# A two-layer hybrid trunk on one core: the delta rule's keys, values and output in three passes of 256 columns, and sums of ones read in turn from two stretches

## The chip, the core and the metric

The kernel runs on one core of a Trainium2 chip. The metric is the device time of one execution in microseconds. Five engines work side by side, each running its own list of instructions in order and waiting for the others by semaphores: PE (TensorE, matrix products into PSUM; its weight loads are shown apart as PEld), DVE (VectorE), ACT (ScalarE), POOL (GpSimd) and SP (SyncE, which here issues the loads of the weights).

## What is computed

Two layers on 256 tokens of 2,048 channels, all in float32: differential attention, then a gated MLP with a causal convolution (the FFN); a gated delta rule, then another such FFN. The change lies in the delta rule:

```python
def gated_deltanet(h, w_in, conv_w, a_log, dt_bias, norm_g, w_out):
    proj = h @ w_in
    qkv, z, b_gate, a_gate = jnp.split(proj, [...], axis=-1)
    qkv = jax.nn.silu(causal_dwconv(qkv, conv_w))
    q, k, v = jnp.split(qkv, [GDN_KEY_DIM, 2 * GDN_KEY_DIM], axis=-1)
    q = l2_norm(q.reshape(b_sz, s_len, GDN_QK_HEADS, GDN_HEAD_DIM).astype(jnp.float32))
    k = l2_norm(k.reshape(b_sz, s_len, GDN_QK_HEADS, GDN_HEAD_DIM).astype(jnp.float32))
    ...
    o = gated_delta_rule(q, k, v, g, beta)
    o = rms_norm(o, norm_g) * jax.nn.silu(z.reshape(b_sz, s_len, GDN_V_HEADS, GDN_HEAD_DIM).astype(jnp.float32))
    return o.reshape(b_sz, s_len, GDN_VALUE_DIM).astype(h.dtype) @ w_out
```

The rule itself (`gated_delta_rule`) solves a unit lower triangular system of 64 x 64 for each chunk of 64 tokens and head, and carries a state from chunk to chunk. There are 16 key heads and 32 value heads of 128.

## The kernel before, in words

**Float32 from two halves.** A float32 matrix product is made of products of a rounded type (`fp32r`). A weight chunk `raw` comes from memory, ScalarE rounds it to `whi` (L88), VectorE keeps the rest as `wlo` (L89). Activations are kept the same way: a main half ah and a small half al, side by side as 2 x 256 tokens. The product is hi·ah + lo·ah + hi·al. In `dense` one *step* (one of kt tiles of 128 input channels, one of 2 tiles of 128 output channels) is a pair: hi against ah and al together, 512 columns, into a whole bank of the accumulator `ps` (L114), then lo against ah, 256 columns, onto its first half (L115). So the first half of the bank holds the main sum and the second half hi·al. Every matmul comes with a load of its weights.

**Reading in turn.** `turns` makes the moving operand alternate between token j and token 128 + j, so the columns of `ps` come out interleaved; `halves` undoes that with a view that steps by two.

**After a dense product.** `merge` (L127) brings the halves together: ScalarE copies the small half out (L134), VectorE adds the main half (L135) and multiplies by the row's norm `rstd` (L136). For output products `add_x` (L242) adds the two halves to the residual x with two VectorE instructions (L245). `total` (L234) sums over the 128 channels of a partition axis with a matmul against ones (L239), the summed operand again in two halves. There it is read straight through.

**The delta rule** (`gdn`) goes over 4 blocks of 4 key heads. For each block: four dense products for keys and queries (`w_in`, 16 x 2 steps each), one for the first values, two products for the gate z (`dense_tok`, L151 to L153, three matmuls of 512 columns a step), three more for the values; then the output products of the block before (`w_out`, 8 products of 8 x 2 steps). The last block's own output closes the layer. Beside it run generators that `tick` steps once per weight chunk: `keys` (norms by L239, ScalarE's logarithms and exponentials at L500 to L506, VectorE's L507, products L514 and L515), `to_tokens` (transposes L604, ScalarE copy L605), `invert` (a loop of small VectorE instructions L542 and L545 that inverts 32 x 32 blocks, closed by two transposes L549 and L551), and `group`, which first joins the blocks (`levels`: L570, L579, L581, L589, L595) and then makes the products L625, the norm of the result (L648, L649, logarithm and exponential L226 and L227, behind a table load L207), the gate multiply L659, the transposes L669 and the operand `oc` of the output product (L672, L673). These small products go to tiles `mp`. The gate z itself leaves `ps` by ScalarE's L704.

**Buffers.** `ps` has two buffers, `mp` four, `raw`, `whi` and `wlo` three each. A chunk of weights is four tiles of 128 input channels for `dense` (8 steps) and two for `dense_tok`.

**What sets the order.** The framework's scheduler puts the instructions of each engine into a list by its own estimate of when each could run. A change of a few matmuls therefore moves others. The weights of every engine's list are consumed in the same sequence, so the place of an instruction can be told by the chunks around it.

Of the kernel before, what the change touches and what calls it, by code (L numbers as in the profile page):

```python
# [10 lines left out]
AF = mybir.ActivationFunctionType  # L11
ALU = mybir.AluOpType
# [4 lines left out]
P = 128  # L17
T = 256
D = 2048
KD = D // P  # L20
EPS = 1e-6
CK = 4
HP, AP, OP = 40, 48, 112
# [3 lines left out]
class Trunk:  # L27
# [71 lines left out]

    def dense(self, w, kt, acts, place, tiles=2, lead=0, dist=(45, 45)):  # L100


        nc = self.nc
        ps = self.banks()
        for k0, nk in self.chunks(kt, CK, lead):
            hi, lo = self.weights(w[:, k0:k0 + nk, :], [(place - x) % P for x in dist])
            steps = [(k, c) for k in range(nk) for c in range(tiles)]
            if k0 + nk == kt:
                steps = [(k, c) for c in range(tiles) for k in range(nk)]
            for k, c in steps:  # L110
# [3 lines left out]
                nc.tensor.matmul(ps[:, c, :], hi[:, k, s], self.turns(a), start=first, stop=False)  # L114
                nc.tensor.matmul(ps[:, c, :T], lo[:, k, s], self.turns(a[:, :1, :]), start=False, stop=last)  # L115
            self.tick()
        return ps
# [8 lines left out]

    def merge(self, ps, u):  # L127

        nc = self.nc
        n = u.shape[1]  # L130
        main, small = self.halves(ps[:, :n])
        t = self.sp.tile([P, 2, T], F32, tag="mt", name="mt", bufs=1)[:, :n]
        v = "p c (q j) -> p c q j"
        nc.scalar.copy(t.rearrange(v, q=2), small)  # L134
        nc.vector.tensor_tensor(u.rearrange(v, q=2), main, t.rearrange(v, q=2), ALU.add)  # L135
        nc.vector.tensor_tensor(u, u, self.rstd.unsqueeze(1).to_broadcast([P, n, T]), ALU.mult)  # L136
# [97 lines left out]
    def total(self, out, parts):  # L234

        n = len(parts)
        for i, p in enumerate(parts):
            for j in range(2):
                last = self.nc.tensor.matmul(out, self.onesr, p[:, j], start=i + j == 0, stop=i + j == n)  # L239
        return last  # L240

    def add_x(self, k, n, ps):  # L242
        x = self.x[:, k:k + n, :].rearrange("p c (q j) -> p c q j", q=2)
        for part in self.halves(ps):
            self.nc.vector.tensor_tensor(x, part, x, ALU.add)  # L245

    def add_out(self, blk, ps, done):

        self.add_x(2 * blk, 2, ps)
# [46 lines left out]
    def attention(self, w_qk, w_v, w_o, nh, dist_ap, ident_ap, qg, kg, lvec, sub, start, done, lambda_init):  # L296

        nc, mp = self.nc, self.mp
        with self.tc.tile_pool(name="at", bufs=1) as at:
# [34 lines left out]
            def normed(ps, gain):  # L334
                r = at.tile([P, 2, T], F32, tag="qkr", name="qkr", bufs=3)
                self.merge(ps, r)
                sq = squares(r)
                qn = at.tile([P, 2, T], F32, tag="qkn", name="qkn", bufs=4)

                def go():  # L340
                    yield
                    pn = mp()
                    self.total(pn, [sq])
                    ri = at.tile([P, 2, T], F32, tag="ri", name="ri", bufs=2)
                    self.rsqrt(ri, pn, P)
# [38 lines left out]
            def values(h, v, aT):  # L384
# [11 lines left out]
                ri = at.tile([P, 2, T], F32, tag="ri", name="ori", bufs=2)  # L396
                self.rsqrt(ri[:, 0, :], pn[:, :T], 2 * P)
                for e in range(2):
# [30 lines left out]
    def gdn(self, w_gate, w_in, w_z, w_out, nb, hb, gate_ap, const_ap, hot_ap, conv_col, ng, done):  # L429
# [12 lines left out]
        with tc.tile_pool(name="gd", bufs=1) as gd:  # L442
# [32 lines left out]
            def keys(hq, c, cc, b0, res):  # L475
# [201 lines left out]
            def out(b, acts):  # L677
                for blk in range(KD // 2):
                    ps = self.dense(w_out[b * (KD // 2) + blk], 2 * hb, lambda k: self.await_(acts, k), OP)
                    self.add_out(blk, ps, done if b == nb - 1 else None)  # L680

# [3 lines left out]
            for b in range(nb):  # L685
# [6 lines left out]
                for op, i in plan + [("v", i) for i in range(1, hb)]:  # L692
                    if op == "k":
                        hq = heads[i]
                        c = convs(lin(self.dense(w_in[hq * 2], KD, self.h_acts, HP)), (hq, nq + hq))
                        self.spawn(keys(hq, c, cc, 2 * i, lqs))
# [9 lines left out]
                    else:  # L706
                        gi = i // gh
                        gr = groups[gi]
                        if i == gr[0]:
# [3 lines left out]
                        hq = heads[i]  # L713
                        c = convs(lin(self.dense(w_in[hq * 2 + 1], KD, self.h_acts, HP)),
                                  (2 * nq + 2 * hq, 2 * nq + 2 * hq + 1))
# [208 lines left out]
```

## Time and profile before

| | |
|---|---|
| median of 3 runs | 2615.27 us (2613.68 to 2615.49) |
| profiled execution | 2612.84 us, its span 2611.1 us |
| mean granted TensorE clock | 0.987 |
| HBM | 476 MB read, 183 GB/s over the span |
| attention and its output, 0 to 320 us | PE busy 309.14 of 320 us |
| FFN of layer 0, in part, 420 to 1060 us | PE busy 640.00 of 640 us |
| delta rule, 1060 to 1892 us | PE busy 794.2 of 832 us |
| FFN of layer 1, 1892 to 2612 us | PE busy 714.42 of 720 us |

The times of matmuls in the trace overlap, since they are pipelined: the distance between the starts of two matmuls is what one of them costs. A window row gives its length, then each engine's busy time and number of instructions, the granted clock, the DMA share and GB/s. The delta rule's sum is that of five windows (64.31, 211.21, 199.02, 205.00 and 114.70 us). The rows on which the prediction rests stand with it.

### The profile page before, as it was taken

To read this page: it belongs to the slowest core of one execution; us is meant where nothing else is said; L and a number is where in the kernel's file an instruction comes from. 1 tells how busy PE (TensorE), PEld (TensorE's weight loads), DVE (VectorE), ACT (ScalarE), POOL (GpSimd) and SP (SyncE) were. 2 spreads that over 40 slices of the span, in tenths; PEclk is the share of its full clock that TensorE was granted. 3 is DMA by queue.
4 is the path that set the end of the run, shared out by engine and by line. 5 is a ranking of instruction groups with operands and counts; after the bars stand their busy time and mean duration, and the time that the engine had idled before them with its cause. 6 is when DMAs were issued, how large, how long until landed. Compare 5 with 4: busy or idle time off the path is not lost.

```text
span 2611.1 us, 41169 instructions
## 1 busy us (share of the span) xinstructions
PE 2557.8 (98%) x15904; PEld 2328.6 (89%) x15904; DVE 1945.4 (75%) x2911; ACT 1510.2 (58%) x2119; POOL 107.2 (4%) x221
## 2 busy tenths in 40 slices
PE   8999999999999999999979999999899999999999
PEld 7998899999999999889969989978799999999998
DVE  7776677778887555789679779779587788776554
ACT  6666656666666444685564674574366666665333
POOL 0000000000000000031021020120100000000000
PEclk9999999999999999999989999999799999999999
DMA  6555565666556666556425446445256556656665
GB/s 211 179 182 177 167 205 199 201 201 201 202 200 203 199 203 200 193 171 194 154 97 194 145 155 200 149 159 170 73 182 202 201 201 201 201 201 206 210 208 169
DMA packets 135412, 480.81 MB, mean 184 GB/s; under 512 B 15408, under 2 KB 18480, under 8 KB 135216
## 3 DMA queue, kind: packets, MB, share of 16 engines
q1 hardware_dynamic: 134064, 475.58, 55.9%
q8 instruction: 124, 2.03, 0.3%
q10 hardware_dynamic: 1152, 2.61, 0.3%
q14 instruction: 72, 0.59, 0.1%
HBM read 476.03 MB, written 2.10 MB: 183 GB/s over the span
## 4 chain that ended last, share of the span: by engine, by line
PE 95%; ACT 2%; DVE 1%; DMA 1%; issue 1%; SPq 0%; ACTq 0%; DVEq 0%
PE ps L114 54%; PE ps L115 27%; PE ps L151 3%; PE ps L153 3%; PE ps L152 3%; PE mp L625 2%; PE mp L239 1%; PE mp L515 1%; ACT whi L88 0%; DMA raw<-w_in 0%; PE mp L595 0%; PE mp L589 0%; DVE wlo L89 0%; PE mp L604 0%; DMA raw<-w_qk 0%
## 5 line engine op out<-in xcount | busy, mean ns | idle before, releaser
L89 DVE TENSOR_TENSOR wlo<-raw,whi 128x1024 fp32r<-128x1024 f32 (+2 forms) x909 | 1104.2, 1215 | 535.4 <-ACT whi L88 521.8
L88 ACT CAST whi<-raw 128x1024 fp32r<-128x1024 f32 (+2 forms) x909 | 945.2, 1040 | 892.2 <-PE ps L114 767.2
L114 PE MATMUL ps<-h,whi 128*128 128x512 f32 x4304 | 1427.0, 385 | 19.1 <-ACT zt L704 9.7
L115 PE MATMUL ps<-h,wlo 128*128 128x256 f32 x4304 | 1182.7, 275 | 2.2 <-DVE wlo L89 2.2
L114 PEld LDWEIGHTS ps<-h,whi 128*128 128x128 f32 x4304 | 818.8, 190 | 135.0 <-ACT zt L704 10.8
L115 PEld LDWEIGHTS ps<-h,wlo 128*128 128x128 f32 x4304 | 831.4, 193 | 5.1 <-DVE wlo L89 3.6
L114 PE MATMUL ps<-ac,whi 128*128 128x512 f32 x1632 | 535.1, 382 | 0.0
L115 PE MATMUL ps<-ac,wlo 128*128 128x256 f32 x1632 | 444.8, 273 | 0.0
L114 PEld LDWEIGHTS ps<-ac,whi 128*128 128x128 f32 x1632 | 308.4, 189 | 43.1 <-issue 0.2
L115 PEld LDWEIGHTS ps<-ac,wlo 128*128 128x128 f32 x1632 | 313.3, 192 | 0.1
L114 PE MATMUL ps<-oc,whi 128*128 128x512 f32 x512 | 171.0, 387 | 0.9 <-DVE oc L673 0.9
L152 PE MATMUL ps<-wlo,h 128*128 128x512 f32 x384 | 145.7, 379 | 1.4 <-DVE wlo L89 1.4
L151 PE MATMUL ps<-whi,h 128*128 128x512 f32 x384 | 146.2, 381 | 0.9 <-ACT whi L88 0.9
L153 PE MATMUL ps<-whi,h 128*128 128x512 f32 x384 | 145.9, 380 | 0.0
L220 DVE SCALAR_TENSOR_TENSOR cv<-u,fcols,cv 128x255 f32<-128x255 f32 (+1 forms) x344 | 142.7, 477 | 0.0
L115 PE MATMUL ps<-oc,wlo 128*128 128x256 f32 x512 | 141.1, 276 | 0.0
L114 PEld LDWEIGHTS ps<-oc,whi 128*128 128x128 f32 x512 | 98.2, 192 | 15.1 <-DVE oc L673 1.3
L115 PEld LDWEIGHTS ps<-oc,wlo 128*128 128x128 f32 x512 | 99.5, 194 | 0.1
L218 ACT ACTIVATE cv<-u,fcols 128x256 f32<-128x256 f32 x172 | 93.9, 593 | 0.6 <-DVE u L136 0.5
L245 DVE TENSOR_TENSOR x<-ps,x 128x512 f32<-128x512 f32 (+1 forms) x114 | 77.0, 676 | 16.5 <-PE ps L115 15.4
L220 DVE SCALAR_TENSOR_TENSOR cv<-u,cols,cv 128x255 f32<-128x255 f32 (+2 forms) x192 | 84.5, 477 | 1.9 <-ACT cv L216 1.8
L136 DVE TENSOR_TENSOR u<-u,rstd 128x512 f32<-128x512 f32 x118 | 81.7, 692 | 3.3
(200 smaller groups left out, 1850.7 us busy)
## 6 DMA issues: line engine op xcount, KB each, us to landing
raw<-w_up SPq DMA_DIRECT2D x344, 512.0 KB, 4.7
raw<-w_down SPq DMA_DIRECT2D x160, 512.0 KB, 3.7
raw<-w_in SPq DMA_DIRECT2D x128, 512.0 KB, 4.6
raw<-w_z SPq DMA_DIRECT2D x64, 512.0 KB, 3.5
raw<-w_out SPq DMA_DIRECT2D x64, 512.0 KB, 4.6
raw<-w_qk SPq DMA_DIRECT2D x63, 512.0 KB, 4.6
raw<-w_v SPq DMA_DIRECT2D x32, 512.0 KB, 3.5
raw<-w_o SPq DMA_DIRECT2D x32, 512.0 KB, 4.7
```

The costliest lines, as they stand in the source:

```text
L88: nc.scalar.copy(hi, raw)
L89: nc.vector.tensor_tensor(lo, raw, hi.bitcast(F32), ALU.subtract)
L114: nc.tensor.matmul(ps[:, c, :], hi[:, k, s], self.turns(a), start=first, stop=False)
L115: nc.tensor.matmul(ps[:, c, :T], lo[:, k, s], self.turns(a[:, :1, :]), start=False, stop=last)
L136: nc.vector.tensor_tensor(u, u, self.rstd.unsqueeze(1).to_broadcast([P, n, T]), ALU.mult)
L151: nc.tensor.matmul(ps[:, c, :], ah, wh, start=first, stop=False)
L152: nc.tensor.matmul(ps[:, c, :], ah, wl, start=False, stop=False)
L153: nc.tensor.matmul(ps[:, c, :], al, wh, start=False, stop=last)
L218: nc.scalar.activation(out, u, AF.Identity, bias=bias, scale=taps[n - 1])
L220: nc.vector.scalar_tensor_tensor(out[:, j:], u[:, :T - j], taps[n - 1 - j], out[:, j:], ALU.mult, ALU.add)
L245: self.nc.vector.tensor_tensor(x, part, x, ALU.add)
L625: nc.tensor.matmul(p[:, v, :], l(v), r[:, v, :], start=i == 0, stop=i == len(terms) - 1)
```

## The change

`dense` gets a switch `wide`. With `wide=False` a step is three matmuls of 256 columns onto the same half bank: hi·ah, lo·ah, hi·al, each read in turn from two stretches as before. The products for keys, queries, values and output of the delta rule use it; attention, the two FFNs, the decay gates and the gate z keep what they had. `merge` of such a product is one VectorE multiply from `ps` by `rstd`, `add_x` one addition. `total` reads its operand in turn, through `pairs`; its result is then interleaved, and `apart` gives the view that undoes it.

```diff
-    def dense(self, w, kt, acts, place, tiles=2, lead=0, dist=(45, 45)):
+    def dense(self, w, kt, acts, place, tiles=2, lead=0, dist=(45, 45), wide=True):
...
+        n = 2 * T if wide else T
...
-                nc.tensor.matmul(ps[:, c, :], hi[:, k, s], self.turns(a), start=first, stop=False)
-                nc.tensor.matmul(ps[:, c, :T], lo[:, k, s], self.turns(a[:, :1, :]), start=False, stop=last)
+                nc.tensor.matmul(ps[:, c, :n], hi[:, k, s], self.turns(a[:, :n // T, :]), start=first, stop=False)
+                nc.tensor.matmul(ps[:, c, :T], lo[:, k, s], self.turns(a[:, :1, :]), start=False, stop=last and wide)
+                if not wide:
+                    nc.tensor.matmul(ps[:, c, :T], hi[:, k, s], self.turns(a[:, 1:, :]), start=False, stop=last)
...
-    def merge(self, ps, u):
+    def merge(self, ps, u, wide=True):
...
+        if not wide:
+            r = self.rstd.rearrange("p (q j) -> p q j", q=2).unsqueeze(1).to_broadcast([P, n, 2, P])
+            nc.vector.tensor_tensor(u.rearrange(v, q=2), main, r, ALU.mult)
+            return
...
-                last = self.nc.tensor.matmul(out, self.onesr, p[:, j], start=i + j == 0, stop=i + j == n)
+                last = self.nc.tensor.matmul(out, self.onesr, self.pairs(p[:, j]), start=i + j == 0, stop=i + j == n)
...
+    def pairs(self, a):
+
+        return a.rearrange("p c t -> p t c") if len(a.shape) == 3 else a.rearrange("p (c t) -> p t c", c=2)
+
+    def apart(self, ps):
+
+        return ps.rearrange("p (t c) -> p c t", c=2)
+
-    def add_x(self, k, n, ps):
+    def add_x(self, k, n, ps, wide=True):
         x = self.x[:, k:k + n, :].rearrange("p c (q j) -> p c q j", q=2)
-        for part in self.halves(ps):
+        for part in self.halves(ps)[:1 + wide]:
             self.nc.vector.tensor_tensor(x, part, x, ALU.add)
...
-                self.merge(ps, u)
+                self.merge(ps, u, False)
...
-                    nc.scalar.activation(sq[:, 0, :], pn[:, :T], AF.Ln, bias=eps128, scale=float(P))
-                    nc.scalar.activation(sq[:, 1, :], pn[:, T:], AF.Ln, bias=self.eps, scale=1.0)
+                    pq, pk = self.apart(pn)[:, 0, :], self.apart(pn)[:, 1, :]
+                    nc.scalar.activation(sq[:, 0, :], pq, AF.Ln, bias=eps128, scale=float(P))
+                    nc.scalar.activation(sq[:, 1, :], pk, AF.Ln, bias=self.eps, scale=1.0)
...
-                        c = convs(lin(self.dense(w_in[hq * 2], KD, self.h_acts, HP)), (hq, nq + hq))
+                        c = convs(lin(self.dense(w_in[hq * 2], KD, self.h_acts, HP, wide=False)), (hq, nq + hq))
```

The two logarithms of attention (L345 and L397) take the view of `apart` in the same way, and the products for values and output get `wide=False` like the keys.

In the scheduler's lists the attention and the FFN stand as before, but in the delta rule nearly every small instruction moves. Three places follow; line numbers of the new kernel are higher (L704 is L721 there, L605 is L621, L542 and L545 are L558 and L561, L549 and L551 are L565 and L567, L570 is L586, L595 is L611, L604 is L620; its dense matmuls are L115, L116 and L118, its merge L138).

ScalarE at the end of the key heads of block 2; `zt<-ps` is the gate leaving the accumulator, `vt` the first values. Before:

```order
L505 ACTIVATE d<-d 128x256
L506 ACTIVATE d<-mp,gc 128x128
L502 ACTIVATE qs<-qs 128x512
L605 COPY vt<-mp 128x2x256
L704 ACT_TABLE_LOAD
L704 ACTIVATE zt<-ps,rstd 128x512 x4
L88 CAST whi<-raw 128x1024 x4
```

Now:

```order
L521 ACTIVATE d<-d 128x256
L522 ACTIVATE d<-mp,gc 128x128
L621 COPY vt<-mp 128x2x256
L721 ACT_TABLE_LOAD
L721 ACTIVATE zt<-ps,rstd 128x512 x2
L88 CAST whi<-raw 128x1024 x5
L721 ACTIVATE zt<-ps,rstd 128x512 x2
L88 CAST whi<-raw 128x1024 x5
```

Both z products left the accumulators in one go, with no rounding of weights between; now five chunks are rounded between the first and the second. It is so in blocks 2, 3 and 4; in block 1 the two were already apart.

VectorE at the end of the inversion of block 4; `x<-ps` is an output product added to the residual, `u<-ps,rstd` the new merge. Before:

```order
L245 TENSOR_TENSOR x<-ps,x 128x512
L542 TENSOR_TENSOR tmp<-X,Ti 128x30
L89 TENSOR_TENSOR wlo<-raw,whi 128x1024
L545 TENSOR_TENSOR Ti<-Ti,tmp 128x30
L549 STREAM_TRANSPOSE ttc<-Ti 128x32x32
L551 STREAM_TRANSPOSE tcc<-Ti 128x32x32
L89 TENSOR_TENSOR wlo<-raw,whi 128x1024
L245 TENSOR_TENSOR x<-ps,x 128x512
```

Now:

```order
L558 TENSOR_TENSOR tmp<-X,Ti 128x30
L561 TENSOR_TENSOR Ti<-Ti,tmp 128x30
L565 STREAM_TRANSPOSE ttc<-Ti 128x32x32
L567 STREAM_TRANSPOSE tcc<-Ti 128x32x32
L89 TENSOR_TENSOR wlo<-raw,whi 128x1024
L138 TENSOR_TENSOR u<-ps,rstd 128x512
L89 TENSOR_TENSOR wlo<-raw,whi 128x1024
L227 SCALAR_TENSOR_TENSOR cv<-u,cols,cv 128x255
```

The inversion ended between the last additions of block 3's output; now it ends while the values of block 4 are merged and convolved, 18 weight chunks earlier.

PE in the inversion levels of block 4. Before:

```order
L579 MATMUL mp<-ttc,pc 32x32 x2
L581 MATMUL mp<-pc,TT 32x32
L589 MATMUL mp<-Ta,lt 64x64 x8
L595 MATMUL mp<-TT,lq 64x64 x8
L570 MATMUL mp<-tcc,lt 32x32 x16
L604 MATMUL mp<-con,cv 128x128 x4
L579 MATMUL mp<-ttc,pc 32x32 x2
```

Now:

```order
L118 MATMUL ps<-oc,whi 128x256
L115 MATMUL ps<-oc,whi 128x256
L116 MATMUL ps<-oc,wlo 128x256
L611 MATMUL mp<-TT,lq 64x64 x8
L586 MATMUL mp<-tcc,lt 32x32 x16
L620 MATMUL mp<-con,cv 128x128 x4
L118 MATMUL ps<-oc,whi 128x256
L115 MATMUL ps<-oc,whi 128x256
```

The levels and the products of block 4's first group followed each other with no dense step between; now steps of block 3's output stand between any two of them.

More of the change, by code (lines that the diff above doesn't have):

```diff
@@ L344, in go @@
                     ri = at.tile([P, 2, T], F32, tag="ri", name="ri", bufs=2)
-                    self.rsqrt(ri, pn, P)
+                    self.rsqrt(ri, self.apart(pn), P)
                     nc.vector.scalar_tensor_tensor(qn, r, gain, ri, ALU.mult, ALU.mult)
@@ L396, in values @@
                 ri = at.tile([P, 2, T], F32, tag="ri", name="ori", bufs=2)
-                self.rsqrt(ri[:, 0, :], pn[:, :T], 2 * P)
+                self.rsqrt(ri[:, 0, :].rearrange("p (c t) -> p c t", c=2), self.apart(pn[:, :T]), 2 * P)
                 for e in range(2):
@@ L678, in out @@
                 for blk in range(KD // 2):
[L679 to L680 removed]
+                    ps = self.dense(w_out[b * (KD // 2) + blk], 2 * hb, lambda k: self.await_(acts, k), OP,
+                                    wide=False)
+                    self.add_out(blk, ps, done if b == nb - 1 else None, False)
             pg = self.dense(w_gate, KD, self.h_acts, HP, tiles=1)
@@ L713, in gdn @@
                         hq = heads[i]
-                        c = convs(lin(self.dense(w_in[hq * 2 + 1], KD, self.h_acts, HP)),
+                        c = convs(lin(self.dense(w_in[hq * 2 + 1], KD, self.h_acts, HP, wide=False)),
                                   (2 * nq + 2 * hq, 2 * nq + 2 * hq + 1))
```

6 lines of the change are left out of this document (3 added, 3 removed).

## The prediction

> **What bounds the kernel now.** I read the page first: busy shares, then the chain of waits.
>
> ```profile
> span 2611.1 us, 41169 instructions
> PE 2557.8 (98%) x15904; PEld 2328.6 (89%) x15904; DVE 1945.4 (75%) x2911; ACT 1510.2 (58%) x2119; POOL 107.2 (4%) x221
> PE 95%; ACT 2%; DVE 1%; DMA 1%; issue 1%; SPq 0%; ACTq 0%; DVEq 0%
> ```
>
> TensorE (PE) is the bound: it holds 95% of the chain. So two questions decide: what PE's own work costs per step of the contraction, and where PE stands still. For the first, the timeline of PE and of its weight loads (PEld) in a plain dense stretch (start, duration):
>
> ```profile
> 699.64 0.38 PE L114 MATMUL ps<-h,whi 128*128 128x512 f32 x1
> 699.86 0.27 PE L115 MATMUL ps<-h,wlo 128*128 128x256 f32 x1
> 699.97 0.38 PE L114 MATMUL ps<-h,whi 128*128 128x512 f32 x1
> ...
> 702.92 0.38 PE L114 MATMUL ps<-h,whi 128*128 128x512 f32 x1
> 699.86 0.19 PEld L114 LDWEIGHTS ps<-h,whi 128*128 128x128 f32 x1
> 699.97 0.19 PEld L115 LDWEIGHTS ps<-h,wlo 128*128 128x128 f32 x1
> ```
>
> Starts, not durations, give the pace: ten pairs from 699.64 to 702.92 are 0.328 us each, 0.22 for the pass of 512 columns and 0.11 for that of 256. Each load starts with the pass before the one that needs it. The load of whi that starts at 699.86 is in use at 699.97, so a load is hidden behind a pass of 256 columns.
>
> For the second question, windows over the places where the slices of the page show a lower clock (length, busy us of PE, PEld, DVE, ACT, POOL, granted clock, DMA share, GB/s). The first row is the end of the key heads of the delta rule's first block, rows two to four those of blocks 2, 3 and 4, the last one the end of the layer:
>
> ```profile
> 1125.00:1161.00 36.00, 35.07 (x175) 30.32 (x174) 30.24 (x51) 31.57 (x48) 15.96 (x29) 1.00 0.54 164
> 1310.00:1351.00 41.00, 27.16 (x120) 21.93 (x119) 28.12 (x57) 29.34 (x48) 10.66 (x32) 0.85 0.28 90
> 1545.00:1555.00 10.00, 6.76 (x35) 5.81 (x34) 7.55 (x15) 9.01 (x16) 5.45 (x17) 0.94 0.53 178
> 1741.00:1764.50 23.50, 16.75 (x76) 13.54 (x75) 18.31 (x34) 18.34 (x32) 9.96 (x26) 0.87 0.42 141
> 1837.40:1890.30 52.90, 40.60 (x397) 36.45 (x396) 23.58 (x43) 18.92 (x31) 4.74 (x8) 0.76 0.18 60
> ```
>
> There PE idles and its granted clock sinks to 0.76 to 0.94. Block 1 loses 0.9 us at full clock. PE's waits, for the whole span (total, times, longest):
>
> ```profile
> PE ps L114 <- ACT zt L704: 9.7, 3, 3.2
> PE mp L669 <- DVE zt L659: 7.6, 3, 3.7
> PE mp L492 <- DVE d L495: 7.0, 3, 3.4
> PE mp L514 <- DVE cv L507: 5.6, 4, 3.3
> ```
>
> All four are latency chains of the delta rule, not weights. These stretches are what the change can win.
>
> **The change part by part. Three passes instead of a pair.** Keys and values are 32 dense products of 16 x 2 steps, the output 32 of 8 x 2: 1,024 + 512 = 1,536 steps. Each goes from 512 + 256 columns to 3 x 256, the same 768 columns, with one more weight load. At 0.11 us a pass (109 ns: a third of 0.328) a triple is 0.328 us: nothing is won or lost. What no row shows is dense passes of 256 going on without a pass of 512 between, so that loads never pause. From below the bound is 0, since the columns are the same. From above the nearest rows are the sums of ones, the one run of such passes, from the chain:
>
> ```profile
> 86.59 0.47 PE mp L239 x2
> 310.69 0.47 PE mp L239 x4
> ```
>
> Four passes of 256, each with a load: 0.118 us each; two of 512: 0.235 each. The two agree per column, so what they lose against 0.11 and 0.22 belongs to the columns (they read one stretch straight through), not to the load. Still, 0.118 is the upper bound: 3 x 118 - 328 = 26 ns, x 1,536 = 40 us. I take 1 ns a triple, 2 us, by the nearer row, the load at 699.86.
>
> The Trainium skill ("TensorE: Matmul & The Clock Gate", The mechanism, What overlaps and what doesn't) has a rule against this change: a weight load overlaps a running matmul only where its row group differs. Here all loads take all rows, so by it each added load would stand bare. The trace disagrees: the load at 699.86 lies wholly beside running passes.
>
> **Sums of ones.** 64 passes of 512 go from 0.235 to the turned 0.22 and 32 of 256 from 0.118 to 0.11: 64 x 16 + 32 x 8 ns = 1.3 us, taken as 1. The logarithms then read every second element of PSUM; the strided copy of L134 (below, 582 ns for 512) prices 256 such elements at no more than the present reads, so nothing.
>
> **Less on VectorE and ScalarE.** (Minimum/median/maximum ns.)
>
> ```profile
> L134 ACT COPY mt<-ps x135: 361/582/592, 28.8 to 2382.0; 128x512 f32<-128x512 f32 x134, 128x256 f32<-128x256 f32 x1
> L135 DVE TENSOR_TENSOR u<-ps,mt x118: 680/683/703, 400.0 to 2383.3; 128x512 f32<-128x512 f32 x118
> L245 DVE TENSOR_TENSOR x<-ps,x x114: 414/684/692, 321.8 to 2607.7; 128x512 f32<-128x512 f32 x110, 128x256 f32<-128x256 f32 x4
> ```
>
> 32 merges lose the copy and the add (0.58 on ScalarE, 0.68 on VectorE; the multiply by rstd stays, now reading PSUM as L135 does) and 32 outputs lose one add of 0.68: 19 us of ScalarE, 44 of VectorE. Seven more activation-table loads in the new order (1.28 each, below) give 9 us of ScalarE back. PE's dense work covers all of it; on its own it is worth nothing.
>
> **The order moves, and that is where the time is.** *Last tail.* Two windows of the instructions on mp alone (inversion levels, group products; busy us of PE, PEld, DVE, ACT): block 3, where they stand between dense steps, and the tail of block 4. Then the dense pairs inside the tail, and the last step of the inversion (first and last start):
>
> ```profile
> 1633.90:1719.30 85.40, 23.46 (x351) 21.53 (x351) 12.18 (x30) 10.69 (x21) 1.00 0.48 152
> 1837.40:1890.30 52.90, 32.87 (x348) 29.32 (x348) 12.35 (x30) 11.42 (x21) 0.76 0.18 60
> L115 PE MATMUL ps<-oc,wlo 128*128 128x256 f32 x24 | 6.8, 285 | 0.0
> L551 DVE STREAM_TRANSPOSE tcc<-Ti x4: 2052/2090/2114, 1229.0 to 1834.1; 128x1024 f32<-128x1024 f32 x4
> ```
>
> Spread out, these matmuls take 23.5 us of PE at full clock; in the tail they and 24 dense pairs (24 x 0.328 = 7.9) fill 52.9. So 52.9 - 23.5 - 7.9 = 21.5 us is latency and lost clock. The tail is late because the inversion ends at 1836 (1834.1 + 2.1), as the output of block 3 runs out. In the new order VectorE ends the inversion before the first of those outputs and PE spreads the levels over them. Between its rows stand the weight splits, so it cannot be late without making the dense steps late. VectorE has the room: 75% busy before, 44 us less now. Saved: 21.5, or 0 if the inversion lags.
>
> *Ends of the key heads in blocks 2 to 4.* The timeline of ScalarE at the end of block 2's keys (in brackets idle time before, and who ended it):
>
> ```profile
> 1347.78 0.59 ACT L605 COPY vt<-mp 128x512 f32<-128x512 f32 x1 [4.66 <-PE mp L604]
> 1348.37 1.28 ACT L704 ACT_TABLE_LOAD   x1
> 1349.66 2.42 ACT L704 ACTIVATE zt<-ps,rstd 128x512 f32<-128x512 f32 x4
> ```
>
> Both gate products z had been finished; with both accumulators full PE had nothing dense left to do and sat through the last heads' chains and these lines. In the new order the second z product stands after L605, as in block 1, and covers that. The three windows lose 13.84 + 3.24 + 6.75 = 23.8 us idle and, by the clock, 0.15 x 27.2 + 0.06 x 6.8 + 0.13 x 16.8 = 6.7: 30.5. Block 1 keeps 0.9; I leave 3 a block for the table loads: 21.5 saved (0 to 30).
>
> *New waits.* In each of eight groups the gate chain runs from the last product to L669. Counted in the orders, about 30 dense steps stood between before (30 x 0.328 = 9.8 us), now 24 to 26 in most groups (7.9 from 24). What they must cover, from the chain of waits and the timeline in block 2's first group:
>
> ```profile
> 1463.67 1.56 PE mp L625 x14
> 1466.82 0.68 DVE L649 TENSOR_REDUCE os<-osq 128x4 f32<-128x512 f32 x1
> 1467.52 1.28 ACT L207 ACT_TABLE_LOAD   x1 [1.03 <-DVE os L649]
> 1471.24 2.15 DVE L659 SCALAR_TENSOR_TENSOR zt<-mp,os,zt 128x128 f32<-128x128 f32 x8
> ```
>
> From 1465.23 to 1473.39 are 8.2 us, 0.3 more than 24 steps; the queues can add as much again: 0.6 x 8 = 5 us lost (0 to 10). Behind L669 on PE stand dense steps, and nothing but PE waits for them.
>
> **Sum**, against the profiled execution's own 2612.84 us (span 2611.1 and 1.7 around it): +2 - 1 - 21.5 - 21.5 + 5 = -37, 2575.8. The median of the runs is 2.4 higher: **2578 us**.
>
> **Rivals.** *A load or read that doesn't keep up* (chance 0.1): triples at the 0.118 of the sums. For it: loads without a pause are not shown at 0.11. Against it: the load at 699.86. 40 instead of 2: 2616, no change; it outweighs the gain from 26 ns a triple.
>
> *The new order is too tight* (0.12), the one on the other side. The scheduler put fewer dense steps between hand-overs of the small matmuls, and PE runs its list in order. Eight groups of some ten hand-overs (levels, transposes, products, gate); if each misses by 0.9 us as the gate chain could, 72 us are lost where I count 5: 2578 + 67 = 2645. It decides from 0.5 us a hand-over. For it: L669 above. Against it: in the old order hand-overs mid-block cost next to nothing: the waits above are at key ends and in the tail.
>
> *Half the gain* (0.15): the last tail is covered, but the key ends stay bound by ScalarE (31.57 busy of 36 in block 1, and table loads are added): 2578 + 21.5 = 2600.
>
> *The load rule* (0.01): each load bare, 1,536 x 0.11 = 169 us on top: 2747. It is the Trainium skill's overlap rule, named above.
>
> **How the numbers follow.** My forecast has 0.62; its own range, from all 30 + 21.5 saved and no new wait to half of either lost, is 2562 to 2589. The range for 8 in 10 takes in the half gain and the first rival: 2556 to 2620. A measurement tells 0.2% (5.2 us) from no change: faster 0.62 + 0.15 + 0.02 from the near ends of the rivals = 0.79; same 0.07, mostly the first rival; slower 0.14.
>
> **What would show it.** Right: the starts of the three passes 0.11 apart; PE's clock near 1.00 at the end of the delta rule; the small matmuls there between dense ones; no wait of dense PE for the gate's L704 (now L721); PE at 99%. Wrong: triples above 0.35 us; PE waiting for VectorE or ScalarE inside blocks over 20 us in all; VectorE over 95% busy for the dozen weight chunks of an inversion.

## The result, and the profile after

The changed kernel takes **2570.49 us** (median of 4 runs, 2570.18 to 2572.15), the kernel before 2615.38 us beside it: a ratio of 0.9831, 95% interval 0.9814 to 0.9848. Faster, by 45 us. Two executions on record ran in a slow state, one of the kernel before (4127.55 us at a granted clock of 0.605) and one of ffn_three (3779.65 us at 0.655), and are left out here. The first page rows, the chain of waits and the row of clocks:

```profile
span 2568.4 us, 44101 instructions
PE 2544.8 (99%) x17440; PEld 2363.4 (92%) x17440; DVE 1912.2 (74%) x2847; ACT 1501.5 (58%) x2094; POOL 110.0 (4%) x221
PEclk9999999999999999999999999999999999999999
PE 90%; DVE 4%; ACT 3%; issue 1%; DMA 1%; POOL 0%; SPq 0%; ACTq 0%; DVEq 0%
```

PE is busy for 13 us less although it runs 1,536 matmuls more, and it idles for 23.6 us of the span (2568.4 - 2544.8) where it idled for 53.3. The clock is at 9 in every slice. Nearly all of the gain lies in the delta rule. Two windows, of the kernel before and of the changed one, from 1110 us (both are then in the keys of block 1, 1.1 us apart) to the last output product:

```profile
1110.00:1929.60 819.60, 782.54 (x5213) 703.69 (x5212) 657.68 (x1121) 483.31 (x689) 102.47 (x209) 0.96 0.48 156
```

```profile
1110.00:1887.00 777.00, 770.33 (x6642) 735.48 (x6641) 626.17 (x1058) 472.13 (x661) 104.33 (x207) 1.00 0.53 165
```

The stretch is 42.6 us shorter. PE's idle time there falls from 37.06 to 6.67 us, that is 30.4; the other 12.2 is busy time: the granted clock is 1.00 instead of 0.96, and what that saves outweighs the matmuls that were added. PE's waits of the changed kernel, the whole span (total, times, longest):

```profile
PE ps L115 <- DVE h L173: 5.9, 1, 5.9
PE ps L116 <- DVE wlo L89: 5.1, 10, 1.3
PE ps L115 <- ACT whi L88: 3.4, 2, 3.0
PE ps L159 <- DVE wlo L89: 2.2, 3, 1.0
PE ps L158 <- ACT whi L88: 1.4, 1, 1.4
```

None of the four waits that the prediction shows is left: not the gate leaving the accumulator (L704, now L721), not the gate multiply (L659, now L675), not the keys' L495 and L507. The first row stands at the start of the kernel. It was there before too (L114 <- DVE h L166, 5.7 us, fourth in the list of before; the prediction's rows leave it out). The other four rows wait for weight halves, `whi` and `wlo`: 12.1 us in all, where the four such rows of before have 8.2. Two rows of 0.4 and 0.2 us end the list.

The places themselves, in windows of the changed kernel that end, to 0.6 us, at the same dense step as those shown of before: first the outputs of blocks 3 and 4, then the ends of the gate z of blocks 2, 3 and 4:

```profile
1782.20:1887.00 104.80, 104.80 (x1022) 104.03 (x1021) 75.88 (x113) 58.11 (x87) 0.00 (x0) 1.00 0.49 161
1294.60:1335.60 41.00, 41.00 (x201) 35.77 (x200) 32.31 (x54) 27.71 (x40) 13.85 (x28) 1.00 0.57 174
1533.00:1543.00 10.00, 10.00 (x48) 8.70 (x47) 9.65 (x19) 4.21 (x4) 0.00 (x0) 1.00 0.69 213
1722.90:1746.40 23.50, 23.39 (x109) 19.87 (x108) 22.18 (x47) 10.33 (x11) 0.00 (x0) 1.00 0.62 181
```

The second row is the place where before PE was busy for 27.16 of 41 us at a clock of 0.85; now it never stands still. The two outputs took 131.6 us before, in this row of the old trace:

```profile
1798.00:1929.60 131.60, 119.30 (x861) 108.37 (x860) 95.25 (x159) 60.89 (x93) 7.67 (x12) 0.88 0.38 129
```

ScalarE's timeline at the end of block 2's keys shows how the wait went:

```profile
1322.43 0.59 ACT L621 COPY vt<-mp 128x512 f32<-128x512 f32 x1 [0.40 <-PE mp L620]
1323.03 1.28 ACT L721 ACT_TABLE_LOAD   x1
1324.33 1.27 ACT L721 ACTIVATE zt<-ps,rstd 128x512 f32<-128x512 f32 x2
1325.48 1.99 ACT L88 CAST whi<-raw 128x1024 fp32r<-128x1024 f32 x2
...
1336.29 1.26 ACT L721 ACTIVATE zt<-ps,rstd 128x512 f32<-128x512 f32 x2
```

The copy L621, the table load and the gate's activations are as long as they were. But only two activations come at 1324, two more 12 us later, and between them PE has a whole z product to run.

### The profile page after: what moved, and what is told of

Read it like the earlier page. It is cut to its first block, busy times and chain, and to the rows that moved or that the text cites. A ratio compares the mean times of both kernels' runs of the same rounds, so it can differ in the third digit from the quotient of the medians.

```text
span 2568.4 us, 44101 instructions
## 1 busy us (share of the span) xinstructions
PE 2544.8 (99%) x17440; PEld 2363.4 (92%) x17440; DVE 1912.2 (74%) x2847; ACT 1501.5 (58%) x2094; POOL 110.0 (4%) x221
## 4 chain that ended last, share of the span: by engine, by line
PE 90%; DVE 4%; ACT 3%; issue 1%; DMA 1%; POOL 0%; SPq 0%; ACTq 0%; DVEq 0%
PE ps L115 47%; PE ps L116 26%; PE ps L118 5%; PE ps L159 2%; PE ps L160 2%; PE ps L158 2%; PE mp L641 2%; DVE wlo L89 2%; ACT whi L88 1%; DVE cv L227 1%; PE mp L246 1%; ACT L487 0%; DMA raw<-w_in 0%; PE mp L611 0%; PE mp L605 0%
## 5 line engine op out<-in xcount | busy, mean ns | idle before, releaser
L115 PE MATMUL ps<-h,whi 128*128 128x512 f32 (+1 forms) x4304 | 1362.4, 358 | 9.4 <-DVE h L173 5.9
L116 PE MATMUL ps<-h,wlo 128*128 128x256 f32 x4304 | 1180.5, 274 | 5.1 <-DVE wlo L89 5.1
L115 PEld LDWEIGHTS ps<-h,whi 128*128 128x128 f32 x4304 | 817.6, 190 | 97.0 <-DVE h L173 5.9
L116 PEld LDWEIGHTS ps<-h,wlo 128*128 128x128 f32 x4304 | 827.5, 192 | 8.4 <-DVE wlo L89 7.3
L115 PE MATMUL ps<-ac,whi 128*128 128x512 f32 x1632 | 535.1, 382 | 0.0
L116 PE MATMUL ps<-ac,wlo 128*128 128x256 f32 x1632 | 444.8, 273 | 0.0
L115 PEld LDWEIGHTS ps<-ac,whi 128*128 128x128 f32 x1632 | 308.5, 189 | 43.0 <-issue 0.2
L116 PEld LDWEIGHTS ps<-ac,wlo 128*128 128x128 f32 x1632 | 313.3, 192 | 0.1
L118 PE MATMUL ps<-h,whi 128*128 128x256 f32 x1024 | 282.4, 276 | 0.0
L118 PEld LDWEIGHTS ps<-h,whi 128*128 128x128 f32 x1024 | 196.5, 192 | 0.5
L115 PE MATMUL ps<-oc,whi 128*128 128x256 f32 x512 | 141.8, 277 | 0.0
L118 PE MATMUL ps<-oc,whi 128*128 128x256 f32 x512 | 141.8, 277 | 0.0
L116 PE MATMUL ps<-oc,wlo 128*128 128x256 f32 x512 | 141.7, 277 | 0.0
L115 PEld LDWEIGHTS ps<-oc,whi 128*128 128x128 f32 x512 | 98.3, 192 | 0.1
L118 PEld LDWEIGHTS ps<-oc,whi 128*128 128x128 f32 x512 | 98.3, 192 | 0.2
L116 PEld LDWEIGHTS ps<-oc,wlo 128*128 128x128 f32 x512 | 98.3, 192 | 0.1
```

Of the source, the lines that this page charges most:

```text
L115: nc.tensor.matmul(ps[:, c, :n], hi[:, k, s], self.turns(a[:, :n // T, :]), start=first, stop=False)
L118: nc.tensor.matmul(ps[:, c, :T], hi[:, k, s], self.turns(a[:, 1:, :]), start=False, stop=last)
```

## The experiments

All ratios are to the kernel before on the same chip, with 95% intervals. Theory A is the prediction's: the gain is the order, that is dense steps beside the latency chains. Edits are shown against the changed kernel.

### One part alone: sums_only, keys_only, out_only, in_only

Each keeps the sums of ones read in turn and makes three passes only for the products named: none, keys, output, keys and values. `merge` and `add_x` of the products that go back to pairs go back with them.

```diff
 # sums_only: no product has wide=False
-  self.dense(w_in[hq * 2], KD, self.h_acts, HP, wide=False)
+  self.dense(w_in[hq * 2], KD, self.h_acts, HP)
 # keys_only: wide=False for w_in[hq * 2] alone
 # out_only:  wide=False for w_out alone
 # in_only:   wide=False for w_in[hq * 2] and w_in[hq * 2 + 1]
```

> The sums of ones read in turn, everything else as before (pairs of 512 and 256). The scheduler's order in the delta rule stays that of before: inversion of block 4 ending with the last additions of block 3's output, both z products leaving together. Theory A (the gain is the moved order; a triple of 256-column passes costs 336 ns against 328): only the sums move, 64 x 16 + 32 x 8 ns = 1.3 us, so 2614. Theory B (the gain is the work taken off VectorE and ScalarE): nothing is taken off, 2614 too. Theory C (the sums hold up PE's chain): most of the 45 us, 2575.

> Three passes for the keys and queries alone (512 of the 1,536 steps), sums in turn; values and output in pairs. In this order the two z products of blocks 2 to 4 are apart (one rounding or more between them), but the inversion of block 4 ends where it ended before (weight chunk 632). Theory A: the ends of the key heads are covered (20 to 30 us won), the last tail is not; the triples cost 512 x 8 ns = 4: 2615 - 1 - 25 + 4 = 2593, and the last 52.9 us window looks as before (PE idle over 10 us there). Theory B: 16 merges of 64 products are lighter, a quarter of the relief: 2615 - 45/4 = 2604.

> Three passes for the output alone (512 steps), sums in turn; keys and values in pairs. In this order block 2 still has both z products leaving together, blocks 3 and 4 have them apart, and the inversion of block 4 ends at weight chunk 629 instead of 632 (614 in the change). Theory A: key ends of blocks 3 and 4 won (10 to 15), block 2's not, 0 to 5 of the tail; triples 4: 2615 - 1 - 13 - 3 + 4 = 2602. Theory B: 32 of the 64 lighter products, half the relief: 2615 - 22 = 2592.

> Three passes for keys and values (1,024 steps), sums in turn; the output in pairs. In this order all z products are apart, and the inversion of block 4 ends at weight chunk 619 (632 before, 614 in the change). Theory A: key ends won as in the change, most of the tail won; triples cost 8 instead of 12 us: between 2566 and 2580. Theory B: half the relief: 2592.

| run | median us | ratio |
|---|---|---|
| sums_only | 2611.98 | 0.9994 (0.9985 to 1.0003) |
| keys_only | 2580.34 | 0.9874 (0.9859 to 0.9889) |
| out_only | 2595.47 | 0.9932 (0.9918 to 0.9947) |
| in_only | 2571.79 | 0.9840 (0.9823 to 0.9856) |

The sums of ones can't be told from nothing by the whole time; the attention, where 64 of these matmuls lie, ends 1.2 us earlier. All of before's waits are still there (shown: the waits of PE in sums_only):

```profile
PE ps L115 <- ACT zt L720: 9.7, 3, 3.2
PE mp L685 <- DVE zt L675: 7.6, 3, 3.7
PE mp L507 <- DVE d L510: 6.9, 3, 3.2
```

keys_only does better than A said. Its windows, first over the outputs of blocks 3 and 4, then over the end of block 2's z:

```profile
1765.50:1897.20 131.70, 119.48 (x861) 108.40 (x860) 95.02 (x160) 60.72 (x93) 7.67 (x12) 0.88 0.40 128
1294.40:1335.40 41.00, 41.00 (x205) 35.96 (x203) 32.98 (x50) 30.10 (x46) 14.36 (x28) 1.00 0.59 176
```

The tail is as before to 0.1 us. The key end is fully covered. So the two gains are separate, and the key ends alone are worth 31.6 us against sums_only by the medians, more than the 21.5 that I had counted. (Between the profiled spans, 2605.9 and 2578.7, it is 27.2, but the profiled execution of sums_only was the second fastest of its ten.) Its gate waits are gone but the multiply's is not:

```profile
PE mp L685 <- DVE zt L675: 7.6, 3, 3.7
```

out_only landed between the two expectations and nearer to the rival's, so its time alone settles nothing. Its window at the end of block 2's z and its gate wait do:

```profile
1312.00:1352.90 40.90, 27.63 (x113) 21.96 (x112) 27.20 (x55) 29.43 (x49) 10.22 (x30) 0.86 0.26 87
```

```profile
PE ps L115 <- ACT zt L721: 3.2, 1, 3.2
```

Block 2 is as bad as before, with one of the three gate waits left; in its lists the z products of block 2 still stand together, those of blocks 3 and 4 apart, and these two were won. The gain follows the order block by block. in_only has nearly all of the gain of the whole change, without touching the output:

```profile
1771.70:1889.80 118.10, 110.23 (x862) 99.44 (x861) 88.33 (x130) 59.62 (x91) 7.06 (x12) 0.97 0.44 143
```

### What a triple costs: ffn_three

```diff
-  ps = self.dense(w_up[j], KD, self.h_acts, HP)
+  ps = self.dense(w_up[j], KD, self.h_acts, HP, wide=False)
-  self.merge(ps, u)
+  self.merge(ps, u, False)
```

> The change, with three passes of 256 for the up products of both FFNs too (2 x 43 x 32 = 2,752 more steps). PE is never idle there, so this prices a triple by itself. Theory 'loads without a pause' (a pass costs 112 ns when its neighbours each bring a load too, so a triple 336 against 328): 2,752 x 8 ns = 22 us, 2592, all of it in the FFN's up stages (11 us each); lighter merges there win nothing. Rival (112 belongs to the delta rule's surroundings: small matmuls, other engines' traffic): 0, 2570.

Measured: 2592.82 us (2588.33 to 2593.70), ratio 0.9919 (0.9903 to 0.9935), span 2591.0. The two FFNs have 2,752 such steps: 2591.0 - 2568.4 = 22.6 us, 8.2 ns a triple, with an idle time of PE of 23.5 us (2591.0 - 2567.5, from its page) against 23.6 in the changed kernel, so no wait is in it; some 1.7 us of it may be a lower clock in the delta rule (0.94 instead of 0.97 during the gate of block 3), which would leave 7.6 ns. PE's timeline in the first FFN (start, duration):

```profile
599.91 0.28 PE L118 MATMUL ps<-h,whi 128*128 128x256 f32 x1
600.02 0.28 PE L115 MATMUL ps<-h,whi 128*128 128x256 f32 x1
600.13 0.28 PE L116 MATMUL ps<-h,wlo 128*128 128x256 f32 x1
...
601.92 0.28 PE L118 MATMUL ps<-h,whi 128*128 128x256 f32 x1
```

18 passes in 2.01 us are 0.1117 us each, a triple 0.335, where a pair took 0.328: 7 ns. Below, 7.6 ns is used.

### Load or columns: lo_half

The product of lo runs over 128 of its 256 columns: half of lo·ah is left out in keys, values and output.

```diff
-  nc.tensor.matmul(ps[:, c, :T], lo[:, k, s], self.turns(a[:, :1, :]), start=False, stop=last and wide)
+  nc.tensor.matmul(ps[:, c, :T if wide else P], lo[:, k, s], self.turns(a[:, :1, :T if wide else P]), start=False, stop=last and wide)
```

> The change, with the second pass of each triple (lo against the main half) cut to 128 of its 256 columns; half of that product is left out. If a pass is bound by its columns (256 / 2.4 GHz plus a few ns, as 0.11 us each suggests), the short pass takes about 56 ns: 1,536 x 55 ns = 85 us less, 2486. If the weight load behind it is the bound, the short pass still takes about 112 ns: 2570 give or take 5 for the order, which hardly moves.

Measured: 2570.6 us (2570.51 and 2570.69), ratio 0.9838 (0.9820 to 0.9857). Nothing is gained from a sixth less of the columns. PE's and PEld's timelines:

```profile
1784.81 0.28 PE L115 MATMUL ps<-oc,whi 128*128 128x256 f32 x1
1784.92 0.22 PE L116 MATMUL ps<-oc,wlo 128*128 128x128 f32 x1
1784.98 0.33 PE L119 MATMUL ps<-oc,whi 128*128 128x256 f32 x1
1785.14 0.28 PE L115 MATMUL ps<-oc,whi 128*128 128x256 f32 x1
```

```profile
1784.81 0.19 PEld L116 LDWEIGHTS ps<-oc,wlo 128*128 128x128 f32 x1
1784.92 0.19 PEld L119 LDWEIGHTS ps<-oc,whi 128*128 128x128 f32 x1
1785.04 0.19 PEld L115 LDWEIGHTS ps<-oc,whi 128*128 128x128 f32 x1
1785.15 0.19 PEld L116 LDWEIGHTS ps<-oc,wlo 128*128 128x128 f32 x1
1785.26 0.19 PEld L119 LDWEIGHTS ps<-oc,whi 128*128 128x128 f32 x1
```

The half pass lets the next one start its record 0.06 us later, but that one then lasts 0.33, and from L115 to L115 are again 0.33 us. The loads keep starting 0.11 to 0.12 apart whatever the columns. These steps, whose passes all bring a load, are paced by the loads.

### Order or freed work: work_back and pairs_order

work_back keeps the passes of the change and gives ScalarE and VectorE back what it took from them: a copy and an addition into a scratch tile in each merge, an addition in each output.

```diff
         if not wide:
+            t = self.sp.tile([P, 2, T], F32, tag="mt", name="mt", bufs=1)[:, :n]
+            nc.scalar.copy(t.rearrange(v, q=2), main)
+            nc.vector.tensor_tensor(t.rearrange(v, q=2), main, t.rearrange(v, q=2), ALU.add)
...
+        if not wide:
+            t = self.sp.tile([P, 2, T], F32, tag="mt", name="mt", bufs=1).rearrange("p c (q j) -> p c q j", q=2)
+            self.nc.vector.tensor_tensor(t, self.halves(ps)[0], x, ALU.add)
```

> The change, with the work that it takes off VectorE and ScalarE put back as unused work: per merge one copy on ScalarE and one addition on VectorE, per output product one addition. The order moves again: z products still apart in all blocks, the inversion of block 4 ends at weight chunk 626 (614 in the change, 632 before), so the levels are spread over block 3's output but the group products still stand uncovered at the end. Theory A (order): key ends won, tail mostly lost, triples 12 us: 2615 - 1 - 32 - 5 + 12 = 2589. Theory B (the freed work itself): nothing freed, triples paid: 2626.

Measured: 2582.09 us, ratio 0.9882 (0.9868 to 0.9896): 31 of the 45 us stay with nothing freed, and A's size was 7 us off. The page's engine row has VectorE where it was, and the outputs of blocks 3 and 4 are the part that is lost again:

```profile
PE 2547.5 (99%) x17440; PEld 2366.2 (92%) x17440; DVE 1943.2 (75%) x2911; ACT 1518.4 (59%) x2127; POOL 117.4 (5%) x221
```

```profile
1776.90:1897.50 120.60, 112.61 (x1119) 109.78 (x1118) 92.66 (x150) 60.13 (x91) 7.73 (x12) 0.97 0.44 141
```

pairs_order does the opposite: pairs of passes everywhere and all of the work of before, but another order of the program.

```diff
 # without wide=False anywhere, as sums_only
 for op, i in plan + [("v", i) for i in range(1, hb)]:
+    if pend and (op, i) == ("z", 1):
+        out(*pend)
+        pend = None
```

> Every dense product has its pair of passes of 512 and 256 columns again, and every merge and residual addition the instructions of the kernel before (sums of ones read in turn, as in sums_only). Only the order of the program is another: in blocks 2 to 4 the output products of the block before are written between the two gate products z, no longer behind the last values. In the scheduler's lists the second z product then stands apart from the first in blocks 2 to 4, and the inversion of block 4 ends some ten weight chunks earlier than before (chunk 622 against 632; 614 in the changed kernel); the products of block 4's two groups still stand together at the end, without dense steps between. Theory A (the gain comes from the place of dense work beside the latency chains, not from fewer passes' work on VectorE and ScalarE): the ends of the key heads of blocks 2 to 4 are covered, 26 us as measured in the changed kernel, and a part of the tail, up to 8 us: 2580 to 2590. Rival B (VectorE's and ScalarE's 44 and 19 us of relief are what makes the difference, the order only shows it): nothing is relieved here, so 2612, as sums_only. The waits tell too: by A none of dense PE for the gate's activations at the ends of keys of blocks 2 to 4, by B 9.7 us of it as before.

Measured: 2598.33 us, ratio 0.9941 (0.9929 to 0.9954); sums_only has 0.9994. Order alone, with nothing freed and no pass changed, wins 13.7 us against sums_only by the medians (11.5 between the profiled spans, 2605.9 and 2594.4). That is neither number: less than A's 22 to 32, and not the nothing of B. The waits of PE tell why:

```profile
PE mp L685 <- DVE zt L675: 13.4, 3, 9.4
...
PE ps L115 <- ACT zt L723: 2.8, 1, 2.8
```

The gate's wait fell from 9.7 to 2.8 us, where A had said none. But the output of block 1 now stood so early that its own operand was late: a transpose L685 waited 9.4 us for the gate multiply with nothing dense ahead of it. In the window of that place PE is again idle for a third of the time, at a clock of 0.85:

```profile
1300.00:1345.00 45.00, 29.64 (x167) 25.81 (x167) 30.29 (x62) 29.22 (x52) 9.81 (x31) 0.85 0.18 60
```

### A version that keeps more: keys_late_tail

Three passes for all keys, for the values of blocks 3 and 4, and for the outputs of blocks 2 and 3; pairs elsewhere (b counts from 0; `lin` and `add_out` are given the same switch for `merge` and `add_x`).

```diff
-  lin(self.dense(w_in[hq * 2 + 1], KD, self.h_acts, HP, wide=False))
+  lin(self.dense(w_in[hq * 2 + 1], KD, self.h_acts, HP, wide=b not in (2, 3)), b not in (2, 3))
-  ps = self.dense(w_out[b * (KD // 2) + blk], 2 * hb, lambda k: self.await_(acts, k), OP, wide=False)
+  ps = self.dense(w_out[b * (KD // 2) + blk], 2 * hb, lambda k: self.await_(acts, k), OP, wide=b not in (1, 2))
```

> Three passes where the order needs them: all keys, the values of blocks 3 and 4, the outputs of blocks 2 and 3; pairs for the values of blocks 1 and 2 and the outputs of blocks 1 and 4 (1,024 steps of 1,536). Order: z products apart, inversion of block 4 ending at weight chunk 618, levels and products of block 4 spread over block 3's output, but the last transposes 16 steps into the last output. Theory A: 512 x 8 = 4 us fewer for passes, blocks 1 and 2 as in the run with keys alone (some 8 us ahead of the change there), about 5 us lost at the last transposes: 2564 (2558 to 2572), faster than the change. Theory B: two thirds of the relief: 2585.

> The changed kernel as it is, beside pairs_order and keys_late_tail_again on one chip. Both theories: 2570, ratio 0.983.

> The kernel of keys_late_tail once more, to be compared with the changed kernel on the same chip. If its lead of 9 us is real: 2561, ratio 0.980, interval below that of after_again. If it was that chip or that call: 2570, within 0.2% of after_again.

Measured: 2561.18 us, ratio 0.9803 (0.9789 to 0.9816). Repeated beside the changed kernel on one chip: 2560.48 (2560.11 to 2560.95) against 2569.93 (2568.91 to 2571.64) for after_again, ratios 0.9797 and 0.9835. The lead of 9 us is real: this version beats both kernels. It has 1,024 triples instead of 1,536, by ffn_three some 4 us. Of the other 5, 1.1 is idle time of PE (2559.4 - 2536.9 = 22.5 us against 23.6) and about 1.7 a clock that does not sink during the gate of block 3 as it does in the changed kernel (0.97 there); the rest was not traced. Its page row and its window over the outputs of blocks 3 and 4:

```profile
PE 2536.9 (99%) x16928; PEld 2345.0 (92%) x16928; DVE 1922.1 (75%) x2871; ACT 1502.6 (59%) x2101; POOL 109.9 (4%) x221
```

```profile
1767.80:1877.90 110.10, 107.42 (x991) 102.17 (x990) 81.91 (x121) 58.75 (x90) 7.65 (x12) 1.00 0.48 153
```

### The tail over all kernels

One reading runs through the kernels in which these two outputs stand together: when the inversion of block 4 begins its last step (the transpose `tcc`, the last start in its group), counted from the first dense step behind the values of block 4 (block 3's output, where the windows shown begin), and how long the outputs of blocks 3 and 4 take. From the group of `tcc` in the changed kernel:

```profile
L567 DVE STREAM_TRANSPOSE tcc<-Ti x4: 2048/2087/2106, 1209.5 to 1768.8; 128x1024 f32<-128x1024 f32 x4
```

| kernel | last step of the inversion, us after the start of output 3 | outputs 3 and 4, us |
|---|---|---|
| before | 1834.1 - 1798.0 = +36.1 | 131.6 |
| keys_only | 1801.3 - 1765.5 = +35.8 | 131.7 |
| out_only | 1813.8 - 1784.3 = +29.5 | 129.0 |
| work_back | 1798.0 - 1776.9 = +21.1 | 120.6 |
| in_only | 1774.1 - 1771.7 = +2.4 | 118.1 |
| keys_late_tail | 1767.4 - 1767.8 = -0.4 | 110.1 |
| lo_half | 1773.3 - 1779.1 = -5.8 | 108.0 |
| changed | 1768.8 - 1782.2 = -13.4 | 104.8 |

The earlier the inversion ends, the shorter the tail, in all eight but for 0.1 us between the first two. It isn't that end alone: in_only and keys_late_tail differ by 3 us in the one and 8 in the other. Their windows show where the 8 lie: PE idles for 7.87 us in the one and 2.68 in the other, at clocks of 0.97 and 1.00. So how the group products are then spread seems to matter too; that was not tried by itself. The triples add 2 us at most to a tail (256 x 7.6 ns).

When the inversion ends hangs on where it stands and on what else VectorE does while it runs. From the first instruction of block 4's inversion to the end of `tcc`, before and now:

```profile
1764.20:1836.10 71.90, 71.90 (x427) 65.72 (x427) 66.31 (x122) 33.89 (x40) 1.64 (x5) 0.97 0.52 176
```

```profile
1725.10:1770.80 45.70, 45.45 (x314) 42.09 (x312) 43.46 (x88) 21.72 (x24) 1.65 (x5) 1.00 0.65 196
```

VectorE is busy for 92% and 95% of these stretches, and the inversion lasts 26 us less, with 88 instructions of VectorE in it instead of 122, 43.5 us of work instead of 66.3. It also starts earlier against the outputs, 57 us ahead of them instead of 34. In work_back it lasts 64.1 us, in pairs_order, where nothing is freed, 55.6: another order can shorten it by itself.

## Why the prediction was right

The forecast was 2578, the time 2570.49: the likeliest case, by its own mechanism and inside its own range of 2562 to 2589. (By the terms that it names, 30 and 21.5 saved and no new wait, the lower end would be 2564 or 2565; the time is inside either way.) Against the profiled span the sum was -37; the measured change is -42.7. Term by term:

**Three passes instead of a pair: mis-sized.** "I take 1 ns a triple, 2 us, by the nearer row, the load at 699.86." By ffn_three a triple costs 7 to 8 ns, so 1,536 of them some 12 us (11.7 at 7.6 ns). That row shows a load hidden behind a pass of 256, but two loads in 0.328 us, never three. lo_half shows what the row could not: loads that follow without a pause start 0.112 us apart, and columns don't matter there. The upper bound, 26 ns from the sums of ones, held. A hint stood in the prediction's own rows: the 14 group products L625 in 1.56 us, 0.111 each with half the columns.

**Sums of ones: -1, measured -1.1** at the end of attention, where sums_only alone shows 1.1 to 1.2. Right.

**Last tail: -21.5, measured about -28.** The two outputs went from 131.6 to 104.8 us, while the stretch from the end of the gate of block 4 to the first of them took 1.7 longer (1763.8 to 1798.0 before, 34.2 us; 1746.3 to 1782.2 now, 35.9), since 96 small matmuls of the tail were spread back into it: -25.1, and 27.8 without the 352 triples in both. The 23.5 us of PE for the small matmuls and the dense pace were the right ingredients: the tail has a clock of 1.00 and no idle time now. Part of what was missed lies ahead of and behind the window of 52.9 us, where I had taken the work for undisturbed; of the kernel before:

```profile
1763.80:1798.00 34.20, 34.20 (x194) 31.09 (x195) 29.29 (x61) 16.15 (x21) 0.00 (x0) 0.93 0.46 149
1890.30:1929.60 39.30, 39.30 (x225) 35.90 (x226) 33.06 (x52) 23.61 (x42) 0.00 (x0) 0.94 0.47 158
```

PE never idles in either, but a clock of 0.94 costs 0.06 x 39.3 = 2.4 us after the chains are over, and 0.93 after the end of the key heads costs 0.07 x 34.2 = 2.4. Here busy is not full speed. The last output, 128 triples of 0.335 or 42.9 us, now takes 43.0.

**Ends of the key heads: -21.5, measured about -25.** The first dense step behind the gate of block 4 starts at 1746.3 instead of 1763.8, 17.5 us earlier, although 1,184 triples, 9.0 us, now lie ahead of it; without them and the sums of ones that is 25.4. keys_only, with 512 triples at 7.6 ns in it, gives 31 by the spans and 35.5 by the medians. Leaving 3 us a block for the table loads was too careful in the windows shown of the changed kernel, which have 0.0, 0.0 and 0.1 us of idle. It was not in block 3: just ahead of its window PE loses 2.9 us idle, 2.4 of it in two waits for weight halves (1.4 for `whi` and 1.0 for `wlo`, at 1496, while ScalarE is at a table load and the keys' logarithms and exponentials), and at a clock of 0.96 some 1.5 more:

```profile
1491.60:1533.00 41.40, 38.48 (x174) 32.00 (x174) 32.29 (x61) 28.80 (x40) 9.69 (x26) 0.96 0.53 155
```

**New waits: +5, measured nothing of the gate chain.** L669 (now L685) is in none of the waits of the changed kernel; the 24 dense steps that I called 0.3 us short were enough. pairs_order has that very wait, 9.4 us at one place, so the mechanism exists, and the scheduler's order of the changed kernel just does not run into it. New waits came elsewhere: those for weight halves rose from 8.2 to 12.1 us, which the prediction did not name.

So an error of 10 us in the triples was more than met by 6.3, 4 and 5 the other way in the three other terms. That they partly cancel, so that the sum is off by only 6 us, is luck; the mechanism and the signs of the two large terms are not.

One premise of the tail was weak: "VectorE has the room: 75% busy before, 44 us less now". That is the mean over the span. During block 4's inversion VectorE was busy for 92% before, and for 30.93 of 31.00 us in one stretch of it (1785.2 to 1816.2). The inversion ends earlier not because there was room, but because it starts earlier and fewer other instructions of VectorE stand between its steps.

The order as the cause is what the runs show best: work_back without the freed work keeps 31 us; pairs_order without freed work or new passes wins 13.7; keys_only and out_only win exactly those places whose order they change. Freed work may have a part: some 12 us lie between work_back and the changed kernel. Whether it acts by its time or by moving the scheduler's choice (the inversion ends 34 us later against the outputs in work_back) stays open. Not tried either: the changed kernel's exact order with pairs in it.

**The rivals.** A load that doesn't keep up was half true: it is the load that paces, at 7 to 8 ns a triple instead of the 26 from which it would outweigh the gain. The too tight order did not come: all PE waits for VectorE and ScalarE inside blocks stay below 13 us, under the 20 named. One warning sign did fire without harm: over the whole inversions of the changed kernel, 17 to 22 weight chunks each, VectorE is busy for 94 to 97%, 43.46 of 45.70 us in block 4, and PE hardly waits there. As a sign it could tell nothing, since before it was 92 to 98%. Half the gain fell with the second window: ScalarE 27.71 us busy of 41, PE 41.00. The rule of the Trainium skill ("TensorE: Matmul & The Clock Gate", The mechanism, What overlaps and what doesn't), that a load overlaps only in another row group, does not hold here. In lo_half's rows each load lies beside a running pass, and by ffn_three's rows three passes with three loads take 0.335 us; with bare loads they would take about twice that. The same section also lets a load go ahead into a background weight buffer, which the prediction left out and which fits the rows.

## What to carry to other kernels

When PE holds 95% of the chain, what is left to win is where it has nothing dense to run beside a latency chain; look in windows for a sunken clock, and count idle time and lost clock together. A change of the form of the matmuls moves the whole order when a scheduler makes the order: compare the lists first and price the moved places, since here they won some 53 us (28 and 25) while the edit's own arithmetic on PE cost 11. And a mean share of an engine says little about the stretch in which a chain runs on it: look at that stretch. When an order is written by hand, look at what the moved dense work itself waits for: pairs_order idles for 15.4 of 45 us at one such place, more than the 13.7 that it won in all.

## What the runs showed of the hardware

Weight loads of 128 columns that follow without a pause start 0.112 us apart, and then set the pace of matmuls of 256 columns (0.335 us a triple with 768 columns, 0.33 with 640 in lo_half) and of 128 (0.111 each for L625). With a pass of 512 between, the same 768 columns take 0.328. The Trainium skill ("TensorE: Matmul & The Clock Gate", LDWEIGHTS (loading the stationary operand)) gives P / 1.2 ns for a load of P columns, so by estimate 107 ns for 128: the right size, 5 ns under what these traces show. That a load follows a load at this pace beside running matmuls of the same rows, and that a pass of 256, 0.109 us where a pass of 512 stands between, is thus just load-bound, was the surprise.
